# Hybrid layer on one core: which quarters of the SwiGLU down projections read stored weight sums, and when their quarters are loaded

## The chip, the cores and the metric

The kernel runs on one core of one Trainium2 chip. The metric is the device time of one execution in microseconds, as the median of several runs. The profile is that of one further execution.

## What is computed

One decoder layer on 256 tokens of width 1024, in float32: a half-weighted SwiGLU, a mixer (a state-space branch beside differential attention), and a second half-weighted SwiGLU, each with RMSNorm before and after. Only the SwiGLUs matter here:

```python
def swiglu(x, w_gate, w_up, w_down):
    return (jax.nn.silu(x @ w_gate) * (x @ w_up)) @ w_down
...
h = h + 0.5 * rmsnorm(swiglu(rmsnorm(h, ffn1_pre_g[l]), ffn1_w_gate[l], ffn1_w_up[l], ffn1_w_down[l]),
                      ffn1_post_g[l])
```

`w_gate` and `w_up` are 1024x2816 and `w_down` is 2816x1024.

## The kernel before, in words

**Float32 from three products.** TensorE multiplies in a reduced format, so every operand is split into a high part and a rest. ScalarE casts the high part (`whi`, `wqh`), VectorE subtracts it from the operand to get the rest (`wlo`, `wql`), and TensorE adds the products high x high, high x rest and rest x high. Each weight therefore costs ScalarE a cast and VectorE a subtraction before TensorE can use it. Raw weights arrive as `raw` tiles of up to 1 MB, issued by SyncE (L330) into three rotating buffers. The split parts, and many other tiles, share a pool `k4` of 29 buffers; a tile waits until one is free.

**Gate and up.** The 2816 inner columns are worked in eleven blocks j of 256. For j from 2 to 10 the loop in `ffn` multiplies a gate block (`pg_f`, `mm_runs`, L430), lets ScalarE apply SiLU, multiplies the up block (`pup_f`), and lets VectorE form their product (L1093). ScalarE casts it to `gh`, VectorE takes the rest `gl` (L410). `take()` asks for the splits of weights three chunks ahead of use.

**Down, as quads.** The first 2048 rows of `w_down` are worked as four quads of 512 rows, each by one Strassen step of seven products (`mm_quads`, L927): the products 1, 2 and 3 use a quarter of the quad's weights as it is, and 5, 7, 6 and 4 use sums of quarters. Each product is six matmuls of 128x512. The remaining 768 rows are three plain chunks (`mm_n`, L765). The strings in `DOWN` give the order: a digit names the quad, `ppp` are the plain chunks. There are two kinds of quad:

- A lower-case `q` is a `Quad`. It loads its two raw chunks, and VectorE makes four sums `wt` (L123) on the way, so a product from a sum costs VectorE a sum and a rest (L137).
- An upper-case `Q` is a `Stored` quad. Its sums were made ahead, during the gate and up loop, by `stored_sums`: GpSimd's queue loads the four quarters (`ws`, L219), VectorE makes the four sums (L222), and GpSimd's queue writes each to DRAM (`sums_f`, L223). When the quad is due, SyncE's queue loads two chunks of sums of 1 MB (5 and 7; 6 and 4) and VectorE only takes the rests (L157). The loaded sums use a pool `u8` with two buffers, so at most two chunks of sums are in the chip at a time, and a third waits until both products of an earlier chunk are split.

The products of a quad run in the order 1, 2, 3, 5, 7, 6, 4, and in the last one 1, 6, 7, 2, 3, 5, 4. After the last quad's product 1, ScalarE copies that accumulator out (`p_f`, L955).

**Order on the engines.** The program's text gives the priority; a scheduler sets the final order on each engine when the program is built, by when it expects each operand and buffer. On the chip each engine runs its list in that order and waits at the head of it.

`store_sums` calls the two generators in `jobs` (one for each stored quad) at given blocks j. Before the change one call loads all four quarters; each later call makes and stores one sum.

Of the kernel before, what the change touches and what calls it, by code (L numbers as in the profile page):

```python
# [45 lines left out]
QK_US = 2.4  # L46
GATE_US = 1.75
SSD_US = 1.55
DOWN = {"f1": "q1 Q2 q3 Q0 ppp", "f2": "q1 Q2 q3 Q0 ppp"}
FIRST, LAST = (1, 2, 3, 5, 7, 6, 4), (1, 6, 7, 2, 3, 5, 4)  # L50
MIXED = (1, 2, 6, 5, 3, 7, 4)
BREAK, STOP = object(), object()
# [3 lines left out]
def tile_hybrid_layer(ctx: ExitStack, tc: tile.TileContext, x, ffn1_pre_g, ffn1_w_gate, ffn1_w_up,  # L56
# [10 lines left out]
    def k4(shape, name, dt=F32):  # L67
        return sb.tile(shape, dt, tag="k4", name=name, bufs=K4_BUFS)
# [4 lines left out]
    def k2(shape, name, dt=F32):  # L73
        return sb.tile(shape, dt, tag="k2", name=name, bufs=K2_BUFS)
# [15 lines left out]
    def bg(shape, name):  # L90
        return ps.tile(shape, F32, tag="bg", name=name, bufs=5)


    class Quad:
# [32 lines left out]
        def split(self, p):  # L127
            load_to(self.i + 2)
            hi = k4([P, 2, 512], f"wqh{self.i}{p}", F32R)
            src = self.quarter(self.PLAIN[p], p) if p in self.PLAIN else self.sum_of(p)  # L130
            nc.scalar.copy(hi, src)  # L131
            rest = self.products[self.products.index(p) + 1:]
            for later in rest[:1] + tuple(q for q in rest[1:2] if p == 3 and q == 4):
                if later in self.SUMS:
                    self.sum_of(later)
            lo = k4([P, 2, 512], f"wql{self.i}{p}", F32R)
            nc.vector.tensor_sub(lo, src, hi.bitcast(F32))  # L137
            self.give_back()
            return lambda kt: hi[:, kt, :], lambda kt: lo[:, kt, :]
# [26 lines left out]
    def chunk(src, shape):  # L166
        units.append((len(chunks), None))
        chunks.append((src, shape))
# [7 lines left out]
    def n_chunk(w, k0):  # L176
        chunk(w[k0:k0 + 2 * P, :].rearrange("(j p) c -> p j c", p=P), [P, 2, D])
# [11 lines left out]
    def stored_quad(w, k0, products, tag):  # L189


        n, first = len(units), len(chunks)
        sums = products[1:3] + products[5:] if products[1] == 6 else products[3:]
        store = dram.tile([P, 4, D], F32, name=f"sums_{tag}{k0}")
        at, todo = {}, [1, 2, *sums[::2]] if sums[0] == 5 else [1, sums[0], 2, sums[2]]
        for i, p in enumerate(todo):
            if p == 1:
                chunk(w[k0:k0 + 2 * P, :512].rearrange("(j p) c -> p j c", p=P), [P, 2, 512])
                at[1] = (i, lambda r: r)
            elif p == 2:  # L200
                n_chunk(w, k0 + 2 * P)
                at[2], at[3] = (i, lambda r: r[:, :, :512]), (i, lambda r: r[:, :, 512:])
            else:
                j = sums.index(p)
                homes[len(chunks)] = tag
                chunk(store[:, j:j + 2, :], [P, 2, D])
                for o in range(2):
                    at[sums[j + o]] = (i, lambda r, o=o: r[:, o, :].rearrange("p (k c) -> p k c", k=2))
        del units[n:]
        q = Stored(first, products, at)  # L210
        units.extend((q, p) for p in products)
        return w, k0, sums, store

    def stored_sums(w, k0, sums, store):

        t = [k4([P, 2, 512], f"ws{k0}{n}") for n in range(4)]
        for n in (1, 0, 3, 2):
            rows = w[k0 + n // 2 * 2 * P:k0 + (n // 2 + 1) * 2 * P, n % 2 * 512:(n % 2 + 1) * 512]
            nc.gpsimd.dma_start(t[n], rows.rearrange("(k p) c -> p k c", p=P))  # L219
        yield  # L220
        for p, n, a, b in ((5, 0, 1, 0), (7, 1, 3, 1), (6, 3, 3, 0), (4, 2, 2, 3)):
            nc.vector.tensor_sub(t[n], t[a], t[b])  # L222
            nc.gpsimd.dma_start(store[:, sums.index(p), :], t[n].rearrange("p k c -> p (k c)"))  # L223
            yield

    down, QUADS, stored = {}, {}, {}
    for tag, plan in DOWN.items():
        QUADS[tag] = [int(c) for c in plan if c.isdigit()]
# [9 lines left out]
    Z0, XS0, B0, C0, DT0, Q0, KK0, V0, G0 = 0, 2048, 4096, 4608, 5120, 5152, 6176, 7200, 8224  # L238
# [264 lines left out]
    def act(*args, **kw):  # L503
        a = nc.scalar.activation(*args, **kw)
        if act_fence[0] is not None:
            tc.add_manual_dep(a.ins, act_fence[0], order, reason="activation table")
        act_since.append(a.ins.name)
        act_last[0] = a.ins
# [532 lines left out]
    def ffn(post_v, tag, ready, turned, then, products):  # L1041
        gu = []

        gh = k4([P, 4, T], f"gh_{tag}0", F32R)
        gl = k4([P, 4, T], f"gl_{tag}0", F32R)
        gu += [(gh[:, m, :], gl[:, m, :]) for m in range(4)]
        sgs = []

        def evict(b, i, acc, r):
            if i == 0:  # L1050
                sgs.append(k2([P, 512], f"sg_{tag}b{b}"))
                act(sgs[b], acc, AF.Silu, scale=1.0 if r is None else r)
            elif r is None:
                nc.vector.tensor_tensor(sgs[b], acc, sgs[b], ALU.mult)
            else:
                nc.vector.scalar_tensor_tensor(sgs[b], acc, r, sgs[b], ALU.mult, ALU.mult)

        def back(b):
            bs = slice(b * P, (b + 1) * P)
            pt_ = bg([P, 4, P], f"pt_{tag}{b}")  # L1060
            for m in range(4):
                nc.tensor.transpose(pt_[:, m, :], sgs[b][:, m * P:(m + 1) * P], ident)
            if 0 in QUADS[tag]:
                nc.scalar.copy(first[0][:, :, bs], pt_)
            split(gh[:, :, bs], gl[:, :, bs], pt_)

        first = [k4([P, 4, T], f"g0_{tag}")] if 0 in QUADS[tag] else []
        products(evict, back)
        back(1)
        del sgs  # L1070
        then()
        sums = {}
        jobs = [stored_sums(*job) for job in stored.get(tag, ())]

        def store_sums(at):

            for i in at:
                if i < len(jobs):
                    next(jobs[i])

        for j in range(2, FF // T):
            if j % 2 == 0:
                gh = k4([P, 4, T], f"gh_{tag}{j}", F32R)
                gl = k4([P, 4, T], f"gl_{tag}{j}", F32R)
            o = (j % 2) * 2
            gu += [(gh[:, o + m, :], gl[:, o + m, :]) for m in range(2)]
            sg = k2([P, 2, T], f"sg_{tag}{j}")
            mm_runs(sg, f"pg_{tag}{j}", take(), act_u, 0)
            act(sg, sg, AF.Silu)
            store_sums({4: (0,), 6: (0,), 8: (1,)}.get(j, ()))  # L1090
            su = k2([P, 2, T], f"su_{tag}{j}")
            mm_runs(su, f"pup_{tag}{j}", take(), act_u, 1)
            nc.vector.tensor_tensor(sg, su, sg, ALU.mult)  # L1093
            split(gh[:, o:o + 2, :], gl[:, o:o + 2, :], sg)
            if j // 2 in QUADS[tag]:
                if j % 2:
                    sums[j // 2] = sums_of(j // 2, even, sg)
                else:
                    even = sg
            if first:  # L1100
                sums[0] = sums_of(0, first[0][:, :2, :], first[0][:, 2:, :])
                del first[0]
            store_sums({2: (0,), 4: (0, 0), 5: (1,), 6: (1, 1), 8: (1,)}.get(j, ()))
        act_table(EXP_LN)
        acc, rest, combine, pairs, begin = mm_quads(gu, sums, tag)
        pg = load_gain(post_v, f"pg_{tag}")

        norms = [{}, {}]

        quarters = (slice(0, 256), slice(256, 512)) if tag == "f2" else ()  # L1110
        tail = [pj(f"tail{i}")[:, :256] for i in range(len(quarters))]

        def half(b, q):
            parts = quarters if b == 1 and q == 1 and quarters else (slice(0, 512),)
            r = rest[b][q]
            for cs in parts:
                behind(nc.vector.tensor_tensor(r[:, cs], acc[b][q][:, cs], r[:, cs], ALU.add), "lo")
            if len(parts) > 1:
                norm_quarters(norms[b], b, q, r, pg, 4.0, tag, parts, tail)
            else:  # L1120
                norm_half(norms[b], b, q, r, pg, 4.0, tag)

        def done(b):
            norm_end(norms[b], b, 4.0, tag)
            ready(b)

        mm_n(acc, gu, done, turned, pairs=pairs, begin=begin,
             taken_all=combine, norms=norms, half=half, quarters=quarters, tail=tail)
# [755 lines left out]
```

## Time and profile before

| What | Value |
|---|---|
| Median of 3 runs | 735.31 us (734.42 to 735.82) |
| Profiled execution | 736.33 us, its span 734.6 us |
| Granted TensorE clock | 0.998 |
| Busy: TensorE, VectorE, ScalarE | 721.9, 639.6, 486.1 us |
| SyncE's loads | 135.80 MB |
| GpSimd's loads and stores | 24.00 MB |

In the profile PE is TensorE, DVE is VectorE, ACT is ScalarE, POOL is GpSimd and SP is SyncE; PEld is the loading of weights into TensorE. A timeline row gives start, duration, engine, line, operation, output and inputs, size and count, and in brackets how long the engine was idle before it and what ended that. Tiles of the first SwiGLU have names with `f1`, of the second with `f2`.

### The profile page before, as it was taken

What the parts mean: (1) busy time and instruction counts of PE and PEld (TensorE: products, weight loads), DVE (VectorE), ACT (ScalarE), POOL (GpSimd) and SP (SyncE); (2) the same over time, 40 slices, a digit from 0 to 9 for tenths busy, and PEclk for the clock granted to TensorE, in tenths of its full rate; (3) what the DMA queues carried; (4) which work ended last, traced back from release to release, by engine and by line L of the source; (5) the groups of instructions that cost most, each with busy time, mean ns of one, the idle gap of its engine ahead of it and who ended that gap; (6) DMA issues with size and microseconds to landing.
All of it is one profiled execution on the core that took longest, in us unless ns stands there. A gap on an engine that the chain in (4) does not pass through costs nothing. (4 is left out here: it accounts for less than half of the span.)

```text
span 734.6 us, 10725 instructions
## 1 busy us (share of the span) xinstructions
PE 721.9 (98%) x4007; PEld 616.0 (84%) x4007; DVE 639.6 (87%) x971; ACT 486.1 (66%) x825; POOL 52.1 (7%) x95
## 2 busy tenths in 40 slices
PE   9999999999999999999999999999999999999996
PEld 7888888778878899999888788888888888888775
DVE  6869998999978999787996998789886799989996
ACT  5646657766867666959975577774764565675672
POOL 4500200000200000000000000000022001000000
PEclk9999999999999999999999999999999999999999
DMA  8977995778583556666574664464544959966851
GB/s 295 271 250 261 340 315 201 285 254 306 158 255 119 163 190 202 220 189 223 147 225 147 205 223 140 149 241 175 172 128 140 318 204 312 320 212 255 291 213 57
DMA packets 100211, 161.00 MB, mean 219 GB/s; under 512 B 3308, under 2 KB 69440, under 8 KB 99136
## 3 DMA queue, kind: packets, MB, share of 16 engines
q1 hardware_dynamic: 92880, 135.80, 55.4%
q0 software_dynamic: 6976, 24.00, 9.6%
q8 instruction: 31, 0.51, 0.3%
q10 hardware_dynamic: 304, 0.53, 0.2%
q14 instruction: 20, 0.16, 0.1%
HBM read 150.85 MB, written 9.47 MB: 218 GB/s over the span
## 5 line engine op out<-in xcount | busy, mean ns | idle before, releaser
L349 DVE TENSOR_TENSOR wlo<-raw,whi 128x1024 fp32r<-128x1024 f32 x204 | 243.3, 1220 | 27.7 <-ACT whi L348 26.9
L348 ACT CAST whi<-raw 128x1024 fp32r<-128x1024 f32 x204 | 206.4, 1049 | 19.8 <-DMA raw<-in_ffn_w_up_dram 8.1
L430 PE MATMUL pg_f<-u_f,whi 128*128 128x512 f32 x288 | 70.0, 392 | 1.6 <-ACT whi L348 1.6
L430 PE MATMUL pup_f<-u_f,whi 128*128 128x512 f32 x288 | 68.7, 391 | 0.0
L430 PEld LDWEIGHTS pg_f<-u_f,whi 128*128 128x128 f32 x288 | 53.6, 188 | 13.8 <-ACT whi L348 2.4
L430 PEld LDWEIGHTS pup_f<-u_f,whi 128*128 128x128 f32 x288 | 52.9, 188 | 10.2
L430 PEld LDWEIGHTS pg_f<-u_f,wlo 128*128 128x128 f32 x288 | 37.2, 191 | 1.6
L430 PE MATMUL pg_f<-u_f,wlo 128*128 128x256 f32 x288 | 37.6, 282 | 0.0
L430 PE MATMUL pup_f<-u_f,wlo 128*128 128x256 f32 x288 | 37.5, 283 | 0.0
L430 PEld LDWEIGHTS pup_f<-u_f,wlo 128*128 128x128 f32 x288 | 35.9, 192 | 0.0
L471 PE MATMUL pgt<-whi,u_mx 128*128 128x512 f32 x128 | 33.1, 393 | 0.0
L157 DVE TENSOR_TENSOR wql<-raw,wqh 128x1024 fp32r<-128x1024 f32 x28 | 32.3, 1219 | 0.5 <-ACT wqh L156 0.5
L420 PE MATMUL pz<-u_mx,whi 128*128 128x256 f32 x128 | 31.6, 284 | 0.0
L419 PE MATMUL pz<-u_mx,whi 128*128 128x256 f32 x128 | 31.6, 284 | 0.0
L409 ACT CAST gh_f<-sg_f 128x512 fp32r<-128x512 f32 x18 | 11.2, 622 | 28.4 <-DVE sg_f L1093 28.4
L430 PE MATMUL pxs<-u_mx,whi 128*128 128x512 f32 x128 | 29.9, 390 | 0.0
L471 PEld LDWEIGHTS pgt<-whi,u_mx 128*128 128x128 f32 x128 | 23.6, 188 | 5.3 <-issue 0.7
L131 ACT CAST wqh<-wt 128x1024 fp32r<-128x1024 f32 x16 | 16.8, 1053 | 16.9 <-DVE wt L123 16.9
L430 PEld LDWEIGHTS pxs<-u_mx,whi 128*128 128x128 f32 x128 | 23.8, 188 | 4.8
L156 ACT CAST wqh<-raw 128x1024 fp32r<-128x1024 f32 x28 | 27.4, 1047 | 0.0
L436 ACT COPY sg_f<-pg_f 128x256 f32<-128x256 f32 x36 | 12.9, 374 | 18.9 <-PE pg_f L430 18.7
L420 PEld LDWEIGHTS pz<-u_mx,whi 128*128 128x128 f32 x128 | 24.5, 192 | 0.2 <-issue 0.2
(481 smaller groups left out, 1673.5 us busy)
## 6 DMA issues: line engine op xcount, KB each, us to landing
raw<-in_w_in_dram SPq DMA_DIRECT2D x40, 1024.0 KB, 5.1
raw<-in_ffn_w_gate_dram SPq DMA_DIRECT2D x20, 1024.0 KB, 6.0
raw<-in_ffn_w_up_dram SPq DMA_DIRECT2D x20, 1024.0 KB, 5.3
raw<-in_ffn_w_down_dram SPq DMA_DIRECT2D x18, 1024.0 KB, 5.5
ws<-in_ffn_w_down_dram POOLq DMA_DIRECT2D x16, 512.0 KB, 7.2
sums_f<-ws POOLq DMA_DIRECT2D x16, 512.0 KB, 3.9
raw<-sums_f SPq DMA_DIRECT2D x8, 1024.0 KB, 7.9
raw<-in_ssd_w_branch_dram SPq DMA_DIRECT2D x8, 1024.0 KB, 5.1
```

What stands on the lines that cost most here:

```text
L131: nc.scalar.copy(hi, src)
L156: nc.scalar.copy(hi, src)
L157: nc.vector.tensor_sub(lo, src, hi.bitcast(F32))
L348: last_cast[0] = behind(nc.scalar.copy(hi, r[:, js, :]), "cast").ins
L349: m = nc.vector.tensor_sub(lo, r[:, js, :], hi.bitcast(F32))
L409: nc.scalar.copy(hi, src)
L419: nc.tensor.matmul(acc[m], wh(j)[:, cs], ah(k0 + j), start=first and j == ks[0], stop=False)
L420: nc.tensor.matmul(acc[m], wh(j)[:, cs], al(k0 + j), start=False, stop=False)
L430: nc.tensor.matmul(to, w_(j)[:, m * P:(m + 1) * P], x_(j), start=first and j == 0, stop=not first and j == KD - 1, skip_group_check=True)
L436: nc.scalar.copy(dst, acc[:, T:])
L471: nc.tensor.matmul(acc, a(k0 + j), b(j), start=first and i == 0, stop=last and i == 11)
```

## The change

```diff
-DOWN = {"f1": "q1 Q2 q3 Q0 ppp", "f2": "q1 Q2 q3 Q0 ppp"}
+DOWN = {"f1": "q1 q2 Q3 Q0 ppp", "f2": "q1 q2 Q3 Q0 ppp"}
...
-        at, todo = {}, [1, 2, *sums[::2]] if sums[0] == 5 else [1, sums[0], 2, sums[2]]
+        at, todo = {}, [*sums[::2], 1, 2] if sums[0] == 5 else [1, sums[0], 2, sums[2]]
...
         for n in (1, 0, 3, 2):
             rows = w[k0 + n // 2 * 2 * P:k0 + (n // 2 + 1) * 2 * P, n % 2 * 512:(n % 2 + 1) * 512]
             nc.gpsimd.dma_start(t[n], rows.rearrange("(k p) c -> p k c", p=P))
-        yield
+            yield
...
-            store_sums({4: (0,), 6: (0,), 8: (1,)}.get(j, ()))
+            store_sums({3: (0,), 4: (0,), 5: (0, 1), 6: (0, 1), 7: (1,), 8: (1,)}.get(j, ()))
...
-            store_sums({2: (0,), 4: (0, 0), 5: (1,), 6: (1, 1), 8: (1,)}.get(j, ()))
+            store_sums({3: (0,), 4: (0, 0), 5: (1,), 6: (0, 1), 8: (1, 1)}.get(j, ()))
```

The four quads keep their order 1, 2, 3, 0. Quad 2, second in the row, now makes its sums on the way; quad 3, third in the row, now reads stored ones. Both loaded quads thus come first and both stored ones last. In the first stored quad the chunks of sums are asked for ahead of the plain quarters. `stored_sums` now ends a step after each quarter's load, so it has eight steps instead of five, and the calls are spread anew over the blocks j = 3 to 8. The number of instructions of each kind stays as it was.

Three places show what this does to the order on the engines.

ScalarE in the first SwiGLU, where block j = 3 ends. `whi` are the high parts of the next gate and up weights, `sg_f` is the gate result (L436 copies it, L504 is SiLU), `su_f` the up result. Before:

```order
L409 CAST sh_501<-sv_500 128x1024
L436 COPY sg_f_517<-pg_f_528 128x256
L436 COPY sg_f_517<-pg_f_529 128x256
L504 ACTIVATE sg_f_517<-sg_f_517 128x512
L436 COPY su_f_567<-pup_f_578 128x256
L348 CAST whi_518<-raw_397 128x1024
L436 COPY su_f_567<-pup_f_579 128x256
L348 CAST whi_522<-raw_397 128x1024
```

And now:

```order
L409 CAST sh_501<-sv_500 128x1024
L436 COPY sg_f_509<-pg_f_520 128x256
L348 CAST whi_510<-raw_397 128x1024
L436 COPY sg_f_509<-pg_f_521 128x256
L348 CAST whi_514<-raw_397 128x1024
L348 CAST whi_565<-raw_407 128x1024
L436 COPY su_f_564<-pup_f_575 128x256
L348 CAST whi_569<-raw_407 128x1024
L504 ACTIVATE sg_f_509<-sg_f_509 128x512
```

The casts of the next weights moved from behind SiLU and a copy of the up result to ahead of both.

VectorE in the first SwiGLU, near the end of the gate and up loop, where the first quad's splits begin. `wql` are rests of the quad's weights, `wt` sums of quarters, `gl_f` the rest of block j = 9's result. Before:

```order
L137 TENSOR_TENSOR wql_1299<-raw_1147,wqh_1297 128x1024
L1093 TENSOR_TENSOR sg_f_1192<-su_f_1242,sg_f_1192 128x512
L410 TENSOR_TENSOR gl_f_1085<-sg_f_1192,gh_f_1084 128x512
L137 TENSOR_TENSOR wql_1303<-raw_1201,wqh_1301 128x1024
L123 TENSOR_TENSOR wt_1307<-raw_1147 128x1024
```

And now:

```order
L1093 TENSOR_TENSOR sg_f_1192<-su_f_1242,sg_f_1192 128x512
L137 TENSOR_TENSOR wql_1303<-raw_1201,wqh_1301 128x1024
L123 TENSOR_TENSOR wt_1307<-raw_1145 128x1024
L410 TENSOR_TENSOR gl_f_1083<-sg_f_1192,gh_f_1082 128x512
L137 TENSOR_TENSOR wql_1309<-raw_1201,wqh_1305 128x1024
```

A rest and a sum of the quad moved in between the product (L1093) and the rest `gl_f`, which needs ScalarE's cast of that product.

ScalarE at the start of the last quad. `wqh` from the first `raw` is that quad's product 1, the two from the next `raw` are its products 6 and 7 (a chunk of stored sums). Before:

```order
L131 CAST wqh_1557<-wt_1545 128x1024
L156 CAST wqh_1567<-raw_1445 128x1024
L156 CAST wqh_1579<-raw_1455 128x1024
L156 CAST wqh_1589<-raw_1455 128x1024
L156 CAST wqh_1599<-raw_1521 128x1024
L955 COPY p_f_1737<-acc_f1p_1426 128x512
```

And now:

```order
L156 CAST wqh_1553<-raw_1431 128x1024
L156 CAST wqh_1567<-raw_1471 128x1024
L955 COPY p_f_1737<-acc_f1p_1426 128x512
L156 CAST wqh_1579<-raw_1533 128x1024
L156 CAST wqh_1589<-raw_1533 128x1024
L156 CAST wqh_1599<-raw_1535 128x1024
```

The copy of product 1's accumulator moved ahead of the casts for products 6 and 7.

## Prediction

> **What bounds the kernel now.** I read the page first, then TensorE's waits, then the gate and quad stages by windows, and last the timelines around each wait.
>
> ```profile
> span 734.6 us, 10725 instructions
> PE 721.9 (98%) x4007; PEld 616.0 (84%) x4007; DVE 639.6 (87%) x971; ACT 486.1 (66%) x825; POOL 52.1 (7%) x95
> ```
>
> TensorE is busy for 98% of the span, so nothing is to be won but its gaps; the list of its waits shows where they are (columns: total us, times, longest).
>
> ```profile
> PE pg_f L430 <- ACT whi L348: 1.6, 2, 0.8
> PE acc_f1p L927 <- ACT wqh L131: 1.4, 3, 0.6
> PE acc_f2p L927 <- ACT wqh L131: 1.4, 3, 0.6
> ```
>
> Two gaps lie in the gate loops, six in the quads: the same four places in each SwiGLU. How large they are is read from starts, since a matmul's end is modelled. In the timelines of the first and the second gate loop:
>
> ```profile
> 50.28 3.81 PE L430 MATMUL pup_f<-u_f,whi 128*128 128x512 f32 x16
> 54.92 3.93 PE L430 MATMUL pg_f<-u_f,whi 128*128 128x512 f32 x16 [0.83 <-ACT whi L348]
> ...
> 587.63 3.82 PE L430 MATMUL pup_f<-u_f,whi 128*128 128x512 f32 x16
> 592.22 3.94 PE L430 MATMUL pg_f<-u_f,whi 128*128 128x512 f32 x16 [0.77 <-ACT whi L348]
> ```
>
> Sixteen matmuls in a row take 3.81 us, the last one 0.39 of it, so one starts every (3.81 - 0.39) / 15 = 0.228 us; I use 0.227. The next block should have started at 50.28 + 16 x 0.227 = 53.91 and did at 54.92: 1.0 us lost, and 0.95 in the second SwiGLU.
>
> ```profile
> L927 PE MATMUL acc_f1p<-wqh,gh_f x24: 389/389/504, 133.1 to 173.6; 128*128 128x512 f32 x24
> L765 PE MATMUL acc_f1p<-whi,gh_f x24: 389/389/476, 174.3 to 191.2; 128*128 128x512 f32 x24
> ...
> 54.92:133.10 78.18, 78.18 (x448) 69.06 (x449) 72.56 (x98) 50.08 (x78) 7.22 (x12) 1.00 0.75 263
> 133.10:174.30 41.20, 39.61 (x169) 31.09 (x168) 40.13 (x40) 30.15 (x34) 0.54 (x1) 1.00 0.83 299
> 670.30:711.60 41.30, 39.73 (x170) 31.17 (x169) 40.24 (x40) 30.13 (x33) 0.54 (x1) 1.00 0.84 301
> ```
>
> The quads run from 133.1 to the plain chunks' first matmul at 174.3, 41.2 us, for 4 x 7 x 6 = 168 matmuls, which take 38.1: 3.1 us lost, and as much in the second SwiGLU. The windows (columns: length, then busy PE, PEld, DVE, ACT, POOL) say why: in the quads DVE is busy for 40.13 of 41.20 us. It was also busy for 72.56 of 78.18 us in the gate loop ahead of it, so it brings little lead into the quads, and TensorE waits for it there through ACT's casts, which wait for DVE's sums. All that can be recovered is 2 x 3.1 + 1.0 + 0.95, 8.1 us.
>
> **The change part by part.** One DVE subtraction on 128x1024 takes this:
>
> ```profile
> 126.81 0.69 DVE L410 TENSOR_TENSOR gl_f<-sg_f,gh_f 128x512 fp32r<-128x512 f32 x1 [0.69 <-ACT gh_f L409]
> 127.75 1.23 DVE L137 TENSOR_TENSOR wql<-raw,wqh 128x1024 fp32r<-128x1024 f32 x1 [0.25 <-ACT wqh L131]
> ...
> 143.13 0.69 DVE L410 TENSOR_TENSOR gl_f<-sg_f,gh_f 128x512 fp32r<-128x512 f32 x1 [0.74 <-ACT gh_f L409]
> 144.08 6.90 DVE L157 TENSOR_TENSOR wql<-raw,wqh 128x1024 fp32r<-128x1024 f32 x6 [0.26 <-ACT wqh L156]
> ...
> 163.51 8.04 DVE L157 TENSOR_TENSOR wql<-raw,wqh 128x1024 fp32r<-128x1024 f32 x7
> ```
>
> Seven in 8.04 us are 1.14 each, less the tail. A product takes TensorE 6 x 0.227 = 1.36 us. A loaded quad needs 7 rests and 4 sums, 11 x 1.14 = 12.5 us of DVE against 9.5 of TensorE, and loses 3.0; a stored quad needs 8.0 and regains 1.5.
>
> *Gate loop.* What ACT did ahead of the stall at 53.9:
>
> ```profile
> 50.98 0.64 ACT L436 COPY sg_f<-pg_f 128x256 f32<-128x256 f32 x2
> 53.03 0.63 ACT L504 ACTIVATE sg_f<-sg_f 128x512 f32<-128x512 f32 x1 [1.41 <-DVE sg_f L437]
> 53.57 0.35 ACT L436 COPY su_f<-pup_f 128x256 f32<-128x256 f32 x1
> 53.82 1.05 ACT L348 CAST whi<-raw 128x1024 fp32r<-128x1024 f32 x1
> ```
>
> The cast stood behind SiLU, which waited 1.41 us for DVE. In the new order it stands behind the first copy: it can run from 51.3 to 52.4, the second half to 53.7, both ahead of TensorE's 53.91. I take the stall as gone in both SwiGLUs, -1.0 and -0.95; at worst it stays, 0. What moves there is the quarters' loads, which no longer take four `k4` buffers at j = 2. SP's own loads profit as well, but nobody on TensorE waits for them there.
>
> *Second quad, now loaded.* In the trace DVE's lead is used up when the second quad's product 2 begins: DVE waits 0.74 and 0.26 for ACT, and its rest starts at 144.08, after TensorE has reached the product. Seen from there, two loaded quads in a row have no stored one between them to regain in. With that lead the second quad would lose 3.0 and the 0.85 that its start lost before: 3.85. Off this goes what DVE gains earlier. The new order fills the two waits at 126.81 and 127.75, 0.69 + 0.25 = 0.94. In all, DVE was idle for 78.18 - 72.56 = 5.6 us in the loop, of which more may be filled; I let 2.4 be the most, which leaves 1.5. Against a gain beyond 0.94 stands the fourth quarter's load: POOL's queue now has it behind the stores of two sums, and each store waits for DVE, so DVE's fourth sum can wait for a load:
>
> ```profile
> ws<-in_ffn_w_down_dram POOLq DMA_DIRECT2D x16, 512.0 KB, 7.2
> ```
>
> Behind that sum on DVE stand the next block's rests. From the second sum to the fourth DVE has about 5.5 us of work (two rests, one sum, four shorter ones) against 7.2 of landing, so up to 1.7 us. I take 2.3 us for the second quad, between 2.9 (with 0.94) and 1.5; the ends are 1.5 and 3.85.
>
> *Third quad, now stored.* Its sums fill both `u8` buffers early, as the second quad's did. It costs TensorE nothing and regains 1.14 against 1.36 a product.
>
> *Last quad.* It needs its sums at its second product, 6, and the buffer for them is free only when the third quad's products 5 and 7 are split; before, a whole loaded quad lay between. Two things bound when product 6 can start. First the load. From the third quad's first rest (just in time) to its product 7's rest DVE needs 4 x 1.14 = 4.6; then come the landing L, a cast of 1.05 and a rest of 1.2; TensorE needs 8 products, 10.9, to get to the same matmul. The wait is 4.6 + L + 2.3 - 10.9 = L - 4.0. Landings of sums in the first and in the second SwiGLU, from the DMA view:
>
> ```profile
> raw<-sums_f SPq DMA_DIRECT2D x1, 1024.0 KB, 5.9
> ...
> raw<-sums_f SPq DMA_DIRECT2D x1, 1024.0 KB, 8.0
> ```
>
> That gives 1.9 and 4.0. Second, ACT's list: the copy of product 1's accumulator now stands ahead of that cast.
>
> ```profile
> 166.35 0.59 ACT L955 COPY p_f<-acc_f1p 128x512 f32<-128x512 f32 x1 [0.20 <-PE acc_f1p L927]
> 166.83 2.00 ACT L156 CAST wqh<-raw 128x1024 fp32r<-128x1024 f32 x2
> ```
>
> The copy begins 0.2 us after TensorE has ended product 1, the cast 0.48 later; with 1.05 and 1.2 the rest is there 2.95 after that end, and product 6's third matmul wants it at 0.45: 2.5 us, whatever the load does. So 2.5 in the first SwiGLU and 4.0 in the second; ends 2.5 and 4.0 in each.
>
> By the fit in the Trainium skill's page DMA: Bandwidth & Descriptors, section Anatomy of one DMA (2.0 us and the bytes at 436 GB/s, made on GpSimd's path), 1 MB would land in an estimated 4.4 us. The load would then bind nowhere, and the sum below would be 1.5 lower, 737.6. The trace's 5.9 and 8.0 stand against it, and I keep them.
>
> *Plain chunks.* The last chunk's load is issued when the last quad's product 3 is split. The chain that ended last has it:
>
> ```profile
> 706.62 5.70 DMA raw<-in_ffn_w_down_dram
> ```
>
> TensorE reached the plain chunks at 711.6, 5.0 later. After a wait at product 6, three more rests (3.4) precede the issue, and TensorE has 0.9 + 5 x 1.36 = 7.7 to go: 4.3. The 0.7 us cost 0.4, ends 0.2 and 0.8, since the chain shows this load late already.
>
> *Sum.* First SwiGLU: 2.3 + 2.5 + 0.4 against 3.1 + 1.0, +1.1. Second: 2.3 + 4.0 + 0.4 against 3.1 + 0.95, +2.65. Together +3.8. The profiled execution took 736.33 us (span 734.6), 1.0 above the median of 735.3, so it would take 740.1; against the median, 739.1. The low ends give (1.5 + 2.5 + 0.2) x 2 - 8.1 = +0.3, 735.6; the high ones (3.85 + 4.0 + 0.8) x 2 - 8.1 = +9.2, 744.5.
>
> **The rivals.** *Faster: the lead pays.* If DVE enters the second quad 3.85 us earlier, that quad's wait and the plain chunks' are gone; the copy's 2.5 stays. Then 2 x 2.5 - 8.1 = -3.1, 732.2. It decides from where the second quad loses less than 0.8 per SwiGLU. For it: 5.6 us of idle DVE in the loop, and the stall of the loop gone. Against it: with the stall TensorE too gains 1.0, which takes DVE's gain back. 0.16.
>
> *Slower still: the quarters land late.* DVE's fourth sum waits, so it gains nothing and the second quad costs 3.85: 739.1 + 2 x 1.55 = 742.2. For it, loads issued from two queues at once in the loop:
>
> ```profile
> ws<-in_ffn_w_down_dram POOLq DMA_DIRECT2D x2, 512.0 KB, 7.2
> raw<-in_ffn_w_up_dram SPq DMA_DIRECT2D x1, 1024.0 KB, 12.2
> ```
>
> The load of up weights took 12.2 us beside the quarters. Against it: single quarters meet less. 0.12. The Trainium skill's page DMA: Bandwidth & Descriptors, section Issuing engines are not separate DMA queues, says that transfers of all issuing engines share the same 16 engines and interleave; by it spreading the quarters moves the delay and does not remove it, and the 12.2 us agree.
>
> *No change.* Gate gain and last quad cancel, as at the low ends: 735.6. 0.12.
>
> **How the numbers follow.** The forecast, +3.8, has 0.60; of it 0.06 may end within 0.2% (1.5 us, about what a measurement of this kernel can tell from no change). Slower: 0.54 + 0.12 = 0.66. Same: 0.12 + 0.06 = 0.18. Faster: 0.16. The range leaves out most of the faster rival and the top of the high ends: 734.3 to 742.8.
>
> **What would show it.** Right: no gap of 1 us at the first block after j = 3; waits in the second quad of 1.5 to 3.85; a wait of 2.5 or more at the last quad's second product, right behind ACT's copy L955, with the sums' load issued some 8 us before it. Wrong: quads of 168 matmuls in less than 41.2 us, or a last quad without that wait. A new gap in the gate loop behind DVE's L222 would speak for the late quarters.

## The result, and the profile after

The changed kernel takes 744.37 us (median of 4 runs, 743.40 to 745.38) where the kernel before took 735.14 beside it: a ratio of 1.0126, 95% interval 1.0107 to 1.0144. The forecast was 739.1, in a range of 734.3 to 742.8: slower was right, but the cost was more than twice what was forecast, 9.2 us instead of 3.8. The profiled execution took 744.97 us, 8.6 more than the one before; all places below are from it.

The head of the page of the changed kernel:

```profile
span 743.3 us, 10721 instructions
PE 724.2 (97%) x4007; PEld 616.4 (83%) x4007; DVE 639.2 (86%) x971; ACT 483.8 (65%) x825; POOL 51.4 (7%) x95
```

TensorE does the same 4007 matmuls; only its gaps are new. Its waits (total us, times, longest):

```profile
PE acc_f1p L927 <- ACT wqh L156: 1.8, 2, 1.6
PE acc_f2p L927 <- ACT wqh L156: 1.8, 2, 1.6
PE acc_f2p L927 <- DVE wql L137: 1.7, 3, 0.6
PE acc_f1p L927 <- DVE wql L137: 1.2, 2, 0.6
PE acc_f1p L927 <- ACT wqh L131: 1.2, 2, 0.6
PE acc_f2p L927 <- ACT wqh L131: 1.2, 2, 0.6
...
PE acc_f2p L765 <- DVE wlo L349: 0.5, 1, 0.5
PE acc_f1p L765 <- DVE wlo L349: 0.5, 1, 0.5
PE pup_f L430 <- DVE wlo L349: 0.5, 1, 0.5
PE acc_f1p L765 <- ACT whi L348: 0.5, 1, 0.5
PE pg_f L430 <- ACT whi L348: 0.4, 1, 0.4
```

Where it stops now is read from the names: second quads (L131, L137), last quads (L156), plain chunks (L765), and one gate loop (L430). The gap of 1 us in the first SwiGLU's gate loop is gone; TensorE's timeline at that place:

```profile
50.10 3.82 PE L430 MATMUL pup_f<-u_f,whi 128*128 128x512 f32 x16
53.76 0.62 PE L430 MATMUL pg_f<-u_f,whi 128*128 128x512 f32 x2
```

50.10 + 16 x 0.227 = 53.73, and the next block starts at 53.76. Quads and plain chunks by first and last starts (times of one: least, median, most; then first and last start):

```profile
L927 PE MATMUL acc_f1p<-wqh,gh_f x24: 388/389/504, 131.6 to 175.3; 128*128 128x512 f32 x24
L765 PE MATMUL acc_f1p<-whi,gh_f x24: 389/389/500, 176.0 to 194.3; 128*128 128x512 f32 x24
L765 PE MATMUL acc_f1p<-wlo,gh_f x24: 389/390/502, 176.5 to 194.7; 128*128 128x512 f32 x24
...
L927 PE MATMUL acc_f2p<-wqh,gh_f x24: 389/389/499, 673.9 to 718.5; 128*128 128x512 f32 x24
L765 PE MATMUL acc_f2p<-whi,gh_f x22: 389/389/496, 719.1 to 735.0; 128*128 128x512 f32 x22
```

The first quads run from 131.6 to 176.0, 44.4 us for 38.1 of matmuls: 6.3 lost, where it was 3.1. The second SwiGLU's take 45.2: 7.1 lost. The plain chunks then take 18.7 us to their last start; before, they took 17.4:

```profile
L765 PE MATMUL acc_f1p<-wlo,gh_f x24: 389/389/497, 174.8 to 191.7; 128*128 128x512 f32 x24
```

By starts, from the first quad's first matmul on, the 8.7 us of longer span are:

| stretch | forecast | measured |
|---|---|---|
| up to the first quads | -1.0 | -1.5 |
| first SwiGLU, quads | +1.7 | +3.2 |
| first SwiGLU, plain chunks | +0.4 | +1.3 |
| from there to the second SwiGLU's quads | -0.95 | +0.5 |
| second SwiGLU, quads | +3.2 | +4.0 |
| second SwiGLU, plain chunks and end | +0.4 | +1.2 |

No stretch but the first came out better than forecast. The row that speaks most plainly is DVE's sum of quarters, from the page's groups (busy us, mean ns; idle us of the engine before it, and what ended it), of the changed kernel and then of the kernel before:

```profile
L222 DVE TENSOR_TENSOR ws<-ws,ws 128x1024 f32<-128x1024 f32 x16 | 19.5, 1222 | 9.9 <-DMA ws<-in_ffn_w_down_dram 9.9
```

```profile
L222 DVE TENSOR_TENSOR ws<-ws,ws 128x1024 f32<-128x1024 f32 x16 | 19.5, 1218 | 0.0
```

DVE, which the quads need most, now stands idle for 9.9 us waiting for quarters, where it never did before. Not all of that is lost, since it waits less for ACT's casts: from 54 us to the first quads its idle time in all grew from 5.6 us (73.47 busy of 79.10) to 7.2 (70.33 of 77.55).

### The profile page after: what moved, and what is told of

Read it like the earlier page. It is cut to its first block, busy times and chain, and to the rows that moved or that the text cites. A ratio compares the mean times of both kernels' runs of the same rounds, so it can differ in the third digit from the quotient of the medians.

```text
span 743.3 us, 10721 instructions
## 1 busy us (share of the span) xinstructions
PE 724.2 (97%) x4007; PEld 616.4 (83%) x4007; DVE 639.2 (86%) x971; ACT 483.8 (65%) x825; POOL 51.4 (7%) x95
## 4 chain that ended last, share of the span: by engine, by line
PE 79%; issue 7%; DVE 5%; DMA 4%; ACT 4%; POOL 1%; DVEq 0%; POOLq 0%; ACTq 0%
PE pg_f L430 8%; PE pup_f L430 8%; PE pxs L430 6%; PE pws L471 6%; PE pgt L471 6%; PE acc_f1p L927 4%; PE pbc L430 3%; PE pk L430 3%; PE pq L430 3%; PE pn_f L487 3%; PE acc_f2p L927 3%; PE pn_mx L471 3%; PE pwd L471 3%; PE pn_f L471 3%; PE acc_f1p L765 2%
## 5 line engine op out<-in xcount | busy, mean ns | idle before, releaser
L430 PE MATMUL pg_f<-u_f,whi 128*128 128x512 f32 x288 | 69.5, 391 | 0.4 <-ACT whi L348 0.4
L430 PE MATMUL pup_f<-u_f,whi 128*128 128x512 f32 x288 | 68.7, 391 | 0.0
L430 PEld LDWEIGHTS pg_f<-u_f,whi 128*128 128x128 f32 x288 | 53.8, 188 | 12.3 <-ACT whi L348 1.3
L430 PEld LDWEIGHTS pup_f<-u_f,whi 128*128 128x128 f32 x288 | 53.0, 188 | 10.2
L430 PE MATMUL pup_f<-u_f,wlo 128*128 128x256 f32 x288 | 37.8, 284 | 0.5 <-DVE wlo L349 0.5
L430 PEld LDWEIGHTS pg_f<-u_f,wlo 128*128 128x128 f32 x288 | 36.9, 191 | 1.4
L430 PE MATMUL pg_f<-u_f,wlo 128*128 128x256 f32 x288 | 37.4, 283 | 0.0
L430 PEld LDWEIGHTS pup_f<-u_f,wlo 128*128 128x128 f32 x288 | 35.9, 192 | 0.7 <-DVE wlo L349 0.7
L430 PE MATMUL pxs<-u_mx,whi 128*128 128x512 f32 x128 | 29.9, 390 | 0.0
L222 DVE TENSOR_TENSOR ws<-ws,ws 128x1024 f32<-128x1024 f32 x16 | 19.5, 1222 | 9.9 <-DMA ws<-in_ffn_w_down_dram 9.9
L430 PEld LDWEIGHTS pxs<-u_mx,whi 128*128 128x128 f32 x128 | 23.8, 188 | 4.8
L156 ACT CAST wqh<-raw 128x1024 fp32r<-128x1024 f32 x28 | 27.0, 1048 | 0.0
L131 ACT CAST wqh<-wt 128x1024 fp32r<-128x1024 f32 x16 | 16.8, 1050 | 14.9 <-DVE wt L123 14.9
```

Of the source, the lines that this page charges most:

```text
L430: nc.tensor.matmul(to, w_(j)[:, m * P:(m + 1) * P], x_(j), start=first and j == 0, stop=not first and j == KD - 1, skip_group_check=True)
```

## The experiments

Every ratio is to the kernel before on the same chip. Theory A: the new order of quads costs what it costs because DVE cannot keep up with two loaded quads in a row. Theory B: the quarters land late, and that makes the rest.

### The two halves of the change, each alone

`plan_alone` has the new `DOWN` and `todo` with the old loads and sums; `loads_alone` the reverse:

```diff
 plan_alone, against the kernel before
-DOWN = {"f1": "q1 Q2 q3 Q0 ppp", "f2": "q1 Q2 q3 Q0 ppp"}
+DOWN = {"f1": "q1 q2 Q3 Q0 ppp", "f2": "q1 q2 Q3 Q0 ppp"}
-        at, todo = {}, [1, 2, *sums[::2]] if sums[0] == 5 else [1, sums[0], 2, sums[2]]
+        at, todo = {}, [*sums[::2], 1, 2] if sums[0] == 5 else [1, sums[0], 2, sums[2]]
 loads_alone, against the kernel before
-        yield
+            yield
-            store_sums({4: (0,), 6: (0,), 8: (1,)}.get(j, ()))
+            store_sums({3: (0,), 4: (0,), 5: (0, 1), 6: (0, 1), 7: (1,), 8: (1,)}.get(j, ()))
-            store_sums({2: (0,), 4: (0, 0), 5: (1,), 6: (1, 1), 8: (1,)}.get(j, ()))
+            store_sums({3: (0,), 4: (0, 0), 5: (1,), 6: (0, 1), 8: (1, 1)}.get(j, ()))
```

> The new order of quads alone (DOWN and todo changed, the quarters loaded four at once and the sums at j = 2, 4, 5, 6, 8 as in the kernel before). Theory A, DVE's account: the second quad's wait is DVE's 6 rests and 4 sums against TensorE's products, so it does not depend on the quarters; the two gate-loop gaps of 1.0 and 0.95 come back, the second quads lose about 4 each, the last quads 2.5 and the plain chunks 1.5 each: 743.5 to 745. Rival B, the late quarters: with the old loads the waits that the new ones caused are gone, so the second quads fall to 2.3 or less and the second SwiGLU's gate loop has no gap but the old one: about 742 to 743.

> The single quarters and the new places of the sums alone, on the old order of quads. If both misses come from the order of quads: the two gate gaps go and nothing else changes, 735.1 - 1.95 = 733.2. If TensorE's gain in the gate loop is only borrowed, because DVE sets the pace in the quads behind it: the gaps go, and the quads lose as much more, 735. If the quarters land late here too (second SwiGLU's gate loop): 1.8 more, 735 to 737.

Measured: the plan alone 1.0133 (1.0111 to 1.0155), the total that A had. Its parts were others: by starts the second quads lost 4.7 each and the last quads 4.0 each, the plain chunks no more than before. The last quads' stop is that of the changed kernel (2.5), and behind it eight matmuls started only every 0.43 us, while the granted clock stood at half for 3.4 us (the window view of `plan_alone`; length, busy PE, PEld, DVE, ACT, POOL, then granted clock):

```profile
170.10:173.50 3.40, 3.40 (x8) 2.76 (x9) 3.40 (x4) 3.40 (x4) 0.00 (x0) 0.51 0.37 151
```

In the changed kernel the clock stayed at 1.00 behind the same stop; what sets this off is not shown. The new `todo` went with `DOWN` in every run, so its own part was not measured.

The loads alone 0.9965 (0.9948 to 0.9981), 2.6 us faster; the first of the three expectations, 733.2 against 735.1 or 0.9974, lies within that interval. TensorE's waits in `loads_alone`, complete but for the start of the program:

```profile
PE acc_f1p L927 <- DVE wql L137: 1.2, 2, 0.6
PE acc_f2p L927 <- DVE wql L137: 1.2, 2, 0.6
...
PE acc_f2p L927 <- DVE wql L157: 0.5, 1, 0.5
```

Both gate gaps are gone and the quads lose less than before too: TensorE's gain in the gate loop is not borrowed from the quads. Thus the change is one good half and one bad half; the bad one costs 1.3 to 1.6% whichever loads go with it. The halves do not add: on the new order of quads the same loads won nothing that is clear of noise (1.0133 to 1.0126). But DVE waits for the quarters here as well:

```profile
L222 DVE TENSOR_TENSOR ws<-ws,ws 128x1024 f32<-128x1024 f32 x16 | 19.5, 1216 | 8.6 <-DMA ws<-in_ffn_w_down_dram 8.6
```

### Does DVE's time in the gate loop reach the quads?

```diff
 no_subtractions, against the changed kernel
-            nc.vector.tensor_sub(t[n], t[a], t[b])
             nc.gpsimd.dma_start(store[:, sums.index(p), :], t[n].rearrange("p k c -> p (k c)"))
```

> The changed kernel without the four subtractions of each stored quad in the gate loops (the quarters are stored as they are). DVE has 8 x 1.22 = 9.8 us less to do in each gate loop and never waits for a quarter. If that work and those waits cost DVE its lead: the second quads' 3.8 and 4.6 go, and the 1.8 of the second SwiGLU's gate loop, 734 to 736. If the lead is capped by something else (ACT's casts, the loads' buffers): only the 1.8 goes, 742.6.

Measured: 1.0001 (0.9989 to 1.0013), the first of the two. In the waits (its lines stand one lower, L926 is L927) the second quad has kept one stop of 0.6 in place of four or five (1.1 us by starts), and the last quad all of its own:

```profile
PE acc_f2p L926 <- ACT wqh L156: 1.8, 2, 1.6
PE acc_f1p L926 <- ACT wqh L156: 1.8, 2, 1.6
...
PE acc_f1p L926 <- ACT wqh L131: 0.6, 1, 0.6
PE acc_f2p L926 <- ACT wqh L131: 0.6, 1, 0.6
```

DVE's time in the gate loop does become lead in the second quads. The last quads' wait has nothing to do with it.

### The second quad's sums on another engine

```diff
 sums_on_pool, against the changed kernel (pool is true for the second quad)
-                nc.vector.tensor_sub(t, self.quarter(n, p), m)
+                (nc.gpsimd if self.pool else nc.vector).tensor_sub(t, self.quarter(n, p), m)
```

> The changed kernel with the second quad's four subtractions on POOL instead of DVE. ACT's copy of product 1 then stands three casts later in its list as well. Theory A: with four times 1.14 us off DVE the second quads lose nothing as long as POOL needs less than two products (2.7 us) for one, and the last quads' 2.5 shrinks to what the load leaves: 733 to 736. If POOL needs more, TensorE waits for POOL and the time stays at 742 or above. Rival B: the waits stay, 743 to 744.

Measured: 1.0138 (1.0117 to 1.0160); nothing was gained. POOL's timeline at the second quad's start, then DVE's:

```profile
136.79 2.40 POOL L123 TENSOR_TENSOR wt<-raw 128x1024 f32<-128x1024 f32 x1 [34.31 <-DVE wql L137]
139.16 3.35 POOL L123 TENSOR_TENSOR wt<-raw,raw 128x1024 f32<-128x1024 f32 x1
```

```profile
136.96 3.31 DVE L137 TENSOR_TENSOR wql<-wt,wqh 128x1024 fp32r<-128x1024 f32 x1
140.19 3.40 DVE L137 TENSOR_TENSOR wql<-raw,wqh 128x1024 fp32r<-128x1024 f32 x1
```

A rest that takes DVE 1.22 us took 3.31 and 3.40 beside POOL's subtractions: it ended 1.1 us after POOL's subtraction had (139.19 and 140.27, 142.51 and 143.59), as if it had run only then. The Trainium skill's page SBUF — State Buffer, section Who interferes with whom, says that a DVE instruction with two SBUF inputs contends with a GpSimd instruction that reads SBUF, and that the pair of ports which the two share is an exclusive lock; this trace agrees. DVE reached the second quad's product 2 17.8 us after the quads' start, in place of 10.1, and the second quads lost 10.0 and 9.8, the last quads nothing. Part of the ten is the clock again: from 146.1 to 156.2 it was granted at 0.50. So the run takes no time off DVE, and does not tell A from B.

### The copy ahead of the last quad's cast

```diff
 copy_later, against the changed kernel (casts: ACT's casts of the stored quads)
-            nc.scalar.copy(p1, bank[1])
+            tc.add_manual_dep(nc.scalar.copy(p1, bank[1]).ins, casts[-3].name, order, reason='later')
```

> The changed kernel with ACT's copy L955 held back until the last quad's first four casts are done; all else as it was. In the changed kernel the sums of the last quad landed at 164.96, the copy ran from 165.52 and the cast from 166.00 on, and TensorE lost 2.5 us at that product in each SwiGLU. If the copy is the whole wait: the 2.5 go, twice, a ratio to the kernel before of about 1.006. If the copy stands on top of the load: the cast can start at the landing, 0.95 earlier, and 1.5 stay: a ratio of about 1.010, and TensorE's wait at the last quad's second product is then for the load of sums. If the load alone sets it: 1.0126 as before.

Measured: 1.0080 (1.0054 to 1.0106). ACT's timeline there, of the changed kernel and then of this one:

```profile
165.52 0.58 ACT L955 COPY p_f<-acc_f1p 128x512 f32<-128x512 f32 x1 [5.97 <-PE acc_f1p L927]
166.00 4.84 ACT L156 CAST wqh<-raw 128x1024 fp32r<-128x1024 f32 x5
```

```profile
165.30 3.90 ACT L156 CAST wqh<-raw 128x1024 fp32r<-128x1024 f32 x4 [5.39 <-DMA raw<-sums_f]
169.10 0.57 ACT L955 COPY p_f<-acc_f1p 128x512 f32<-128x512 f32 x1
```

With the copy behind, the cast starts when the sums land. By starts the last quad loses 1.4 in the first SwiGLU and 1.2 in the second, in place of 2.5 in each: the copy stood on top of the load, the middle expectation. The ratio fell by more than these 2.4 us; in this execution the second SwiGLU's gate loop has no gap either, since DVE waited there for its last quarter for 0.80 us and not 2.55. DVE's list there is the changed kernel's, so that gap comes and goes with the landing. The second quads lost 4.4 each.

### The fourth quarter ahead of the stores

POOL's queue in `loads_alone` and in the changed kernel held the fourth quarter behind two stores, and each store waits for DVE. POOL's timeline in the changed kernel, with the second of the two stores (the load landed 8.0 us later):

```profile
634.40 0.56 POOL L223 DMA_DIRECT2D sums_f<-ws  x1 [0.89 <-DVE ws L222]
634.96 0.72 POOL L219 DMA_DIRECT2D ws<-in_ffn_w_down_dram  x1
```

One step is moved so that it goes out ahead:

```diff
 loads_ahead, against loads_alone; plan_loads_ahead, against the changed kernel
-            store_sums({3: (0,), 4: (0,), 5: (0, 1), 6: (0, 1), 7: (1,), 8: (1,)}.get(j, ()))
+            store_sums({3: (0,), 4: (0, 0), 5: (0, 1), 6: (0, 1, 1), 7: (1,), 8: (1,)}.get(j, ()))
-            store_sums({3: (0,), 4: (0, 0), 5: (1,), 6: (0, 1), 8: (1, 1)}.get(j, ()))
+            store_sums({3: (0,), 4: (0,), 5: (1,), 6: (0, 1), 8: (1,)}.get(j, ()))
```

In POOL's order the fourth load (ws_561) moves from behind two stores to ahead of all four:

```
 L219 DMA ws_562<-in_ffn_w_down_dram 128x2x512
+L219 DMA ws_561<-in_ffn_w_down_dram 128x2x512
 L223 DMA sums_f_66<-ws_559 128x1024
 L223 DMA sums_f_66<-ws_560 128x1024
-L219 DMA ws_561<-in_ffn_w_down_dram 128x2x512
 L223 DMA sums_f_66<-ws_562 128x1024
```

> The single quarters on the old order of quads, with the fourth quarter of each stored quad asked for ahead of the first store in POOL's queue (4: (0, 0) ahead of SiLU's products and 6: (0, 1, 1), the sums after them). With the loads alone DVE waited 8.6 us for fourth quarters and the quads still lost 2.0 and 2.9. If that waiting is lead that the quads lack: both go, and the ratio falls from 0.9965 to about 0.991. If the quarters' buffers are then taken from the casts too early: a gap in the gate loop comes back and the ratio is 0.996 or more.

> The changed kernel with the same fourth quarters ahead of the stores; the order of quads is the changed one. Theory: the late fourth quarter costs DVE 9.9 us, of which the second SwiGLU's gate loop loses 1.8 and each second quad up to 2.5; last quads and plain chunks keep their 2.5 and 1.5. Then the ratio falls from 1.0126 to between 1.003 and 1.010. Rival: the quads cost what they cost because of their order alone: only the 1.8 goes, 1.010.

Measured: 0.9927 (0.9904 to 0.9951) on the old order, 1.0057 (1.0034 to 1.0079) on the new one. DVE's waits for quarters are gone; the group in `plan_loads_ahead`:

```profile
L222 DVE TENSOR_TENSOR ws<-ws,ws 128x1024 f32<-128x1024 f32 x16 | 19.5, 1217 | 0.0
```

So 0.7% of the changed kernel's time, 5 us (3.8 between the two profiled spans), was the place of one load in a queue, more than the rival's 1.8. What it did in the second quads shows in one number: how long after the quads' first matmul DVE reaches the rest of the second quad's product 2. The timelines of TensorE and DVE, of the changed kernel and then of `plan_loads_ahead`:

```profile
131.55 0.39 PE L927 MATMUL acc_f1p<-wqh,gh_f 128*128 128x512 f32 x1
...
141.64 1.23 DVE L137 TENSOR_TENSOR wql<-raw,wqh 128x1024 fp32r<-128x1024 f32 x1 [0.25 <-ACT wqh L131]
```

```profile
131.92 0.39 PE L927 MATMUL acc_f1p<-wqh,gh_f 128*128 128x512 f32 x1
...
141.16 1.22 DVE L137 TENSOR_TENSOR wql<-raw,wqh 128x1024 fp32r<-128x1024 f32 x1 [0.26 <-ACT wqh L131]
```

That lag was 141.64 - 131.55 = 10.1 and is 141.16 - 131.92 = 9.2. From there DVE has 10 operations of 1.14 to do up to product 4's rest, and TensorE 13 products and 2 matmuls from the start: lag + 11.45 - 18.16, and 0.4 for four slow restarts, is lag - 6.3. By starts the second quads lost 3.8 and 3.0. In ten second quads of five kernels with this order (lags of 9.2 to 11.3) the loss was lag - 6.3 to within 0.1, and so it was in the two of `no_subtractions` (lags 7.4 and 7.5, losses 1.1 and 1.2). `plan_alone`, with the old loads, has a lag of 11.0 and a loss of 4.7 in both. Theory A holds, with its number; B holds as a cause of the lag. On the old order the quads of `loads_ahead` lose 1.2 and 2.2, but in the profiled execution the first SwiGLU's plain chunks lost 4, over 1 us of it at a granted clock of 0.50 (176.1 to 179.5).

### Both mends, and a version that beats both kernels

`plan_ahead_copy` is `plan_loads_ahead` with the copy held back as above. In `gain_early` the gain's load is asked for ahead of the quads, on top of `loads_ahead`:

```diff
+        pg = load_gain(post_v, f"pg_{tag}")
         acc, rest, combine, pairs, begin = mm_quads(gu, sums, tag)
-        pg = load_gain(post_v, f"pg_{tag}")
```

> The changed kernel with both mends: the fourth quarters asked for ahead of the stores, and the copy L955 held back until the last quad's first four casts. If the late quarters and the copy are separate costs, their savings add: from 1.0126, 0.7% for the quarters and 2 x 1.05 us (0.3%) for the copy, 1.003, with second quads of 3.0, last quads of 1.5 and plain chunks of 1.3 to 1.6 left. If both are the same wait seen twice: 1.0057 as with the quarters alone. The order of quads alone would then still cost what is left above the old order with the same loads (0.9927).

> The single quarters ahead of the stores on the old order of quads, and the gain's load (L738) asked for before the quads instead of behind them. In the profiled execution of the one without this, the first SwiGLU's last plain chunk landed after 8.4 us beside the gain's load, issued in the same moment, and TensorE lost 4 us there; in the second SwiGLU it landed after 5.6 and nothing was lost. If that meeting is what costs: no loss at the plain chunks, and a ratio of 0.988 to 0.992. If the gain held early takes a buffer that the quads need: 0.993 or more.

Measured: `plan_ahead_copy` 1.0031 (1.0015 to 1.0046), as if the savings added. Its profiled execution does not bear that out: the last quads lose 2.0 and 0.7, but the second quads 3.2 and 5.0 (lags of 9.5 and 11.3), so quads in all are where they were. The trace shows where the second SwiGLU's longer lag came from. On DVE, ACT and the DMA queues `plan_ahead_copy` runs the list of `plan_loads_ahead` but for the copy; at the same place in the gate loop, ACT's and DVE's timelines of `plan_loads_ahead` and then of `plan_ahead_copy`:

```profile
626.35 1.05 ACT L348 CAST whi<-raw 128x1024 fp32r<-128x1024 f32 x1 [3.61 <-DMA raw<-in_ffn_w_up_dram]
627.43 1.23 DVE L349 TENSOR_TENSOR wlo<-raw,whi 128x1024 fp32r<-128x1024 f32 x1 [1.70 <-ACT whi L348]
```

```profile
627.34 1.05 ACT L348 CAST whi<-raw 128x1024 fp32r<-128x1024 f32 x1 [4.67 <-DMA raw<-in_ffn_w_up_dram]
628.42 1.23 DVE L349 TENSOR_TENSOR wlo<-raw,whi 128x1024 fp32r<-128x1024 f32 x1 [2.76 <-ACT whi L348]
```

Up weights, loaded beside four quarters, landed after 13.2 us in place of 12.2, and DVE waited 1.1 us longer for them; at an earlier load of up weights it waited 2.69 in place of 1.83. TensorE waited at neither place, but these 1.9 us make up nearly all of the 2.0 by which the lag grew (11.3 against 9.3).

`gain_early` 0.9905 (0.9884 to 0.9926), 1% faster than the kernel before. The last plain chunk's load in the first SwiGLU, with what was issued beside it, in `loads_ahead` and then here (the DMA view; last column us to landing):

```profile
raw<-in_ffn_w_down_dram SPq DMA_DIRECT2D x1, 1024.0 KB, 8.4
pg_f<-in_ffn_post_g_dram POOLq DMA_DIRECT2D x1, 512.0 KB, 7.4
```

```profile
raw<-in_ffn_w_down_dram SPq DMA_DIRECT2D x1, 1024.0 KB, 4.8
```

With the gain's load out of the way it landed in 4.8, and TensorE lost nothing at the plain chunks in either SwiGLU. Between the two the ratio's intervals overlap, and their medians are both 730.36 us (beside 735.84 and 736.60 of the kernel before), so that the step itself wins anything is not shown.

## Why the prediction was right in sign and wrong in size

The forecast missed about 5 us: the second quads cost 3.8 more than its sum had, a new gap in the gate loop 1.8 and the plain chunks 1.6; the last quad of the second SwiGLU cost 1.5 less and the other stretches 0.8 less. That the measured +9.2 is also what the prediction's high ends give is chance: they had 4.0 in both last quads and no new gap.

- **Gate loop, -1.0 and -0.95.** The gap went in both, as forecast. That a new one would come in the second SwiGLU was a rival's mark ("a new gap in the gate loop behind DVE's L222"), and it came. TensorE's timeline and then DVE's there:

```profile
644.35 0.64 PE L430 MATMUL pup_f<-u_f,wlo 128*128 128x256 f32 x4
645.48 1.70 PE L430 MATMUL pup_f<-u_f,wlo 128*128 128x256 f32 x12 [0.49 <-DVE wlo L349]
```

```profile
643.06 1.23 DVE L222 TENSOR_TENSOR ws<-ws,ws 128x1024 f32<-128x1024 f32 x1 [2.55 <-DMA ws<-in_ffn_w_down_dram]
```

  DVE's rests stood behind that sum, and TensorE lost 1.8 there by starts, at this place and at the next block. The prediction saw the queue (the fourth load behind two stores) and allowed up to 1.7 of DVE's time for it; four waits cost 9.9, some 2.5 each, and the forecast's own sum took only part of one, as lost lead.
- **Second quad, 2.3: measured 3.8 and 4.6.** This step failed, twice. The base of 3.85 was put together from the stage's averages; from the lag in the trace of before, 144.08 - 133.1 = 11.0, it is 4.7, which is what `plan_alone` lost. And DVE did come 2.44 us earlier, just the 2.4 that was allowed, but TensorE came 1.5 earlier too, and only the difference of 0.9 is lead. The prediction held this against its rival ("with the stall TensorE too gains 1.0") and not against its own sum. 4.7 - 0.9 = 3.8. In the second SwiGLU, where the late quarters and the new gap came on top, the lag was 10.9 and no more than 0.1 of lead was won: 4.6. (The prediction's list of TensorE's waits lacks two of 0.2 us at the second quads' product 2; the 0.85 that was lost there is in its sum.)
- **Third quad, nothing.** Right: no stop is in it.
- **Last quad, 2.5 and 4.0: measured 2.5 in both.** The copy's bound was right to the tenth. The 4.0 took a landing of 8.0 from another place of the old trace; in the first SwiGLU of `copy_later` the sums took 5.9 to land. By the prediction's L - 4.0 that leaves 1.9; 1.4 was left (1.2 in the second SwiGLU), since the third quad's first rest was not just in time but done 0.5 us before TensorE wanted it.
- **Plain chunks, +0.4: measured +1.3 and +1.1.** The mechanism was right, the landing too short. TensorE reached the plain chunks 4.3 us after the issue of the last chunk's load (171.74 to 176.00), as forecast, but in the first SwiGLU that load took this:

```profile
raw<-in_ffn_w_down_dram SPq DMA_DIRECT2D x1, 1024.0 KB, 6.6
```

  Before, it took 5.95 there and 5.70 in the second SwiGLU, where it now takes 6.4: 0.7 more in each, and with the 0.7 of lead that is gone, 1.4. The gain's load now goes out 0.7 us ahead of it (171.03), where before both went out at once. In `plan_alone` it goes out 0.75 us behind, the chunk lands after 4.9 (4.8 in the second SwiGLU), and nothing is lost; but TensorE also came later there, 5.8 us after the issue.
- **The rule that was weighed.** That spreading the quarters moves the delay of other loads and does not remove it was right; the prediction's own "SP's own loads profit as well" was not. The DMA issues of gate weights before and in the changed kernel (up weights went from 5.3 to 6.3):

```profile
raw<-in_ffn_w_gate_dram SPq DMA_DIRECT2D x20, 1024.0 KB, 6.0
```

```profile
raw<-in_ffn_w_gate_dram SPq DMA_DIRECT2D x20, 1024.0 KB, 7.4
```

  In the gate loop TensorE does not wait for these loads, but DVE does, through ACT's casts, and in `plan_ahead_copy` such waits became lag. DVE's waits for quarters, however, came from the place in the queue and not from the landing: in `plan_loads_ahead` quarters took 7.4 us to land, in the changed kernel 7.3, and yet those waits were gone.
- **The rivals.** Late quarters, priced at 1.55 per SwiGLU, cost about 2.5 by the ratios; the faster one failed as its "against" said. On top of both stands the order itself: with all mends to the loads it is still 9.6 us slower than the old one (1.0057 against 0.9927).

## What to carry to other kernels

Lead is a difference: when a change lets the slow engine start earlier, subtract what it lets the fast one start earlier, and count the loss from one measured distance between them, not from averages of a stage. A load for which the fast engine never waits can still take lead from the slow one. A load that shares an in-order queue with stores is as late as the engine that the stores wait for; place it ahead of them before anything else is tuned. And when a change has two halves, price each alone: here one was worth 0.35% (0.7% when mended) and hid behind another that cost 1.3%.

## What the runs showed of the hardware that was not expected

Two-input subtractions of 128x1024 on POOL and on DVE do not run side by side: DVE's took 3.31 and 3.40 us beside POOL's in place of 1.22, and POOL's own took 2.4 to 3.4. Behind some stops of TensorE the granted clock fell to half: for 3.4 us in `plan_alone` (both last quads) and `loads_ahead`, for 10.2 us in `sums_on_pool` (both second quads), with a matmul every 0.43 us in place of 0.227; the changed kernel's stops did not bring it on. Of two loads issued in the same moment, 1 MB and 512 KB, the larger landed after 8.4 us in `loads_ahead`, where alone it took 4.8 at the same place; but the other pairs of the same two loads, in the kernel before, in `loads_alone` and in the second SwiGLU of `loads_ahead`, landed the larger after 5.6 to 6.0, so the 8.4 is not due to the second load alone.
